# Finer steps for the running sums, a stream's operands made one phase later, and a last projection that stays in PSUM

## The chip, the cores and the metric

The kernel runs on one NeuronCore of a Trainium2 chip, in one launch. Its time is the device time of an execution, in microseconds (us); lower is better. The profile names the engines PE (TensorE matmul; PEld is its weight load), DVE (VectorE), ACT (ScalarE), POOL (GpSimd) and SP (SyncE).

## What is computed

Two blocks of a model, all in float32, on 256 image tokens of width 1024. The first block has two layers with attention, a recurrent branch and a gated feed-forward net. The second has two layers whose shifts, scales and gates come from vectors `c` (and `c_ctx` for a second stream of 256 context tokens); this is the part that the change touches:

```python
def second_block(x, c, ctx, c_ctx, w_ada, b_ada, norm_g, ...):
    h, hc = x, ctx
    for layer in range(DEPTH):                      # 2 layers
        with_ctx = layer < DEPTH - 1                # the context stream leaves after layer 0
        sh_m, sc_m, gt_m, sh_f, sc_f, gt_f = ada_chunks(c, w_ada[layer], b_ada[layer])
        csh_m, ...                         = ada_chunks(c_ctx, w_ada[layer], b_ada[layer])
        xm = modulate(h, g_pre_m, sh_m, sc_m)       # rms norm * (1 + scale) + shift
        cm = modulate(hc, g_pre_m, csh_m, csc_m)
        y, yc = even_mixer(xm, cm, ...) if layer % 2 == 0 else odd_mixer(xm, cm, ...)
        h = h + gt_m * rms_norm_2(y, g_post_m)
        f = conv_ffn(modulate(h, g_pre_f, sh_f, sc_f), w_up[layer], ..., w_down[layer])
        h = h + gt_f * rms_norm_2(f, g_post_f)
        if with_ctx: ...                            # the same two steps for hc
    return h

def ada_chunks(cvec, w, b):                         # w: 1024 x 6144
    m = jax.nn.silu(cvec) @ w + b
    return jnp.split(m[..., None, :], 6, axis=-1)

def odd_mixer(xm, cm, w_qkv, q_g, k_g, w_out, cos, sin, with_ctx):
    # queries of 16 heads from xm; keys and values of 4 heads from xm and cm;
    # norm and rope of queries and keys, softmax attention, @ w_out

def conv_ffn(x, w_up, conv_w, conv_b, w_down):      # 2816 = 22 * 128 hidden channels
    h = conv of 3 tokens over (x @ w_up) + conv_b
    a, g = jnp.split(h, 2, axis=-1)
    return (jax.nn.silu(g) * a) @ w_down
```

## The kernel before

**Products.** Every float32 matrix is split into a high and a low part of the matmul's own type, and a product is three matmuls (`mm3`, L357 to L361): high by high, low by high, high by low. Weights come in 362 blocks of 512 KB and eight of 384 KB (`load`, L324): one DMA on SP's queue into `raw` (3 buffers), ACT copies to `whi`, DVE subtracts to `wlo` (4 buffers each). `self.ahead` blocks are asked for ahead of use. With `self.parts` at 4 the two copies are made in quarters of 128x256.

**Engines.** A tile scheduler places the program's instructions on the engines' queues and puts in semaphore waits. Each queue is then executed in its own order. `high_priority(HP)` lets a piece be placed ahead of what the program wrote before it; `issue_after(i)` holds it back until instruction `i` has been placed, so that it stands behind it.

**Streams.** Stream 0 is the image, stream 1 the context. `prepare` (L1043, its steps from L1047) makes a mixer's or FFN's operands for one stream out of its state `hn` (two tiles of 128 tokens): four ACT squares with row sums (L1056), a reciprocal root of seven small DVE operations for each tile (`rsqrt1`, L410 to L416), four scaled ACT copies (L1061), and for each of eight chunks two PE transposes (L1067), an ACT scale and shift into `pt` (L1070), a DVE cast (L1071) and a DVE subtraction (L1072). `post` (L1075) adds a projection's result to `hn`: two squares (L1080), two products with the gate row (L1084), `rsqrt1`, two updates (L1089).

**Running sums.** The vectors `ada` of the second block are sums over 1024 inputs. For eight of the twelve pieces DVE makes them, while PE does other work: `ada_sums` (L510) loads eight tiles `wadb` of 128x1024 (512 KB, on POOL's DMA queue, 3 buffers), multiplies each by one column for each stream and adds it to `asum` (L524 for the first, L526 for the others). When the eight are done PE sums over partitions (L533, L545) and DVE adds the bias (L535, or L546 and L547 for the gate rows). Four pieces need both streams, and the first four of the eight to be done are these; the last four need stream 0 alone. `ada_sums` is a generator, and yields once for each `wadb` tile; `sum_step` takes steps of it.

**The second block's first FFN** (`second_ffn`, L1230) has 22 hidden chunks in groups of 2, 4, 4, 4, 4 and 4. `up(c)` makes chunk `c` of both streams (48 matmuls of 512 columns into two of four PSUM tiles `up`), and conv, silu and split: on DVE two additions for each half (L1185, L1187), L1219, L1220 and L1094. After the ups of a group, `down` does the products of the group before: 96 matmuls of 512 columns into eight PSUM tiles `acc` (three buffers), each of which DVE adds to `y` (L1271). Sums are taken in each up from the third on: three steps behind the split (L1240 to L1242), which are six sums in a row where both streams are wanted. After the last group, `down` ends with `post` and `prepare` for stream 0 and then for stream 1 (L1261).

**The last mixer** (`odd_mixer`) makes five queries (stream 0 alone, `query`, L1465), two keys of both streams (`keys`, L1439), values, and then attention with three more queries between. A query ends in ACT's `qraw` and `qsq`, four small PE products (L1472), the rope product (L1430), and on DVE L1432 to L1434, L1094 and a root of ten small operations. Its projection (`out_products`, L1144) is done in two halves of four operand chunks: the first in the middle of the attention, copied to `y` by ACT (L1157); the second at the end, added to `y` by DVE (L1160); then `post` and `prepare` of the last FFN.

Of the kernel before, what the change touches and what calls it, by code (L numbers as in the profile page):

```python
# [7 lines left out]
F32 = mybir.dt.float32  # L8
# [11 lines left out]
KD = 8  # L20
# [262 lines left out]
class Net:  # L283
    def __init__(self, tc, I, O):
        self.tc, self.nc, self.I, self.O = tc, tc.nc, I, O
        self.es, self.es2 = ExitStack(), ExitStack()
        pool = lambda name, **k: self.es.enter_context(tc.tile_pool(name=name, **k))
        self.keep = pool("keep", bufs=1)
        self.wp = pool("wp", bufs=4)
        self.sp = pool("sp", bufs=2)  # L290
        self.ps = pool("ps", bufs=1, space=PSUM)
        self.dr = pool("dr", bufs=1, space=bass.MemoryType.DRAM)
        self.loaded = {}
        self.nload = 0
# [12 lines left out]
        self.ada_bufs = 5  # L307

# [15 lines left out]
    def load(self):  # L324
# [9 lines left out]
        for j in range(self.parts):  # L334
            cs = slice(n * j // self.parts, n * (j + 1) // self.parts)
            nc.scalar.activation(hi[:, cs], raw[:, cs], AF.Copy)  # L336
            nc.vector.tensor_tensor(lo[:, cs], raw[:, cs], hi[:, cs].bitcast(F32), op=ALU.subtract)  # L337
# [19 lines left out]
    def mm3(self, out, a, b, start, stop):  # L357
        mm = self.nc.tensor.matmul
        mm(out, a[0], b[0], start=start, stop=False)  # L359
        mm(out, a[0], b[1], start=False, stop=False)  # L360
        mm(out, a[1], b[0], start=False, stop=stop)  # L361
# [43 lines left out]
    def rsqrt1(self, a, b, name):  # L405
# [10 lines left out]
        nc.vector.scalar_tensor_tensor(y, u, R0, y, op0=ALU.add, op1=ALU.mult)  # L416
# [93 lines left out]
    def ada_sums(self):  # L510
# [4 lines left out]
        for u, (l, p) in enumerate(SUMS):  # L515
            streams = (0, 1) if l == 0 or p < 2 else (0,)
            acc = [self.adap.tile([128, 1024], F32, tag="asum", name="asum", bufs=3) for _ in streams]
            for k in range(KD):
# [8 lines left out]
                if k + 1 < KD:  # L527
                    yield
# [22 lines left out]
    def sum_step(self, n=1):  # L551
        for _ in range(n):
            next(self.sum_gen, None)
# [370 lines left out]
    def first_ffn(self, l, gp, other):  # L924
# [10 lines left out]
        def up(c):  # L935
# [14 lines left out]
            if not last and 2 <= c < 2 + KD:  # L950
                with self.tc.issue_after(self.mark.ins):
                    self.sum_step()
# [144 lines left out]
    def second_block(self):  # L1097
        xs = self.xs
        for l in range(DEPTH):
# [3 lines left out]
            with a as mp, b as self.ph:  # L1103
# [8 lines left out]
                with self.tc.high_priority(HP):  # L1112
                    for t in range(2):
                        self.post(t, fin.y(t), B[0], junk, scratch)
                    self.prepare(l, 1, 0, xs, 0, junk, scratch, "sc")
# [57 lines left out]

    def conv_up(self, l, xs, mp, S, between=None):
# [6 lines left out]
        def conv(ps, c, tag):  # L1181
# [5 lines left out]
            nc.vector.scalar_tensor_tensor(a[:, :, :255], b[:, :, 1:], cw[:, 88 + c:89 + c], a[:, :, :255],  # L1187
                                           op0=ALU.mult, op1=ALU.add)
# [12 lines left out]
        def up(c):  # L1201
# [5 lines left out]
            self.parts = 1  # L1207
            if c in held:
# [21 lines left out]
    def second_ffn(self, l, xs, mp, between):  # L1230
# [7 lines left out]
        def up(c):  # L1238
            r = up0(c)
            if c >= 2:  # L1240
                with self.tc.issue_after(self.mark.ins):
                    self.sum_step(3)  # L1242
            return r

        def down(ys, g):
            final = g + 1 == len(FFN2_GROUPS)
            if final:
# [6 lines left out]
                for s in range(2):  # L1254
# [6 lines left out]
                    self.prepare(l + 1, 0, s, nxt, 256 * s, scratch, room, "up")  # L1261
                return
            for i in range(2):
                w = self.weights(len(ys) // 2)
                for t in range(4):
# [4 lines left out]
                    else:  # L1270
                        nc.vector.tensor_tensor(y[t, i], y[t, i], ps, op=ALU.add)  # L1271
# [4 lines left out]
    def second_ffn_last(self, l, xs, mp, B):  # L1276
        y = self.ffn_whole(self.conv_up(l, xs, mp, 1))
        for t in range(2):
            self.post(t, y[t], B[0], lambda: self.chunk(mp, "th", 2), lambda: self.chunk(mp, "a", 2))
# [135 lines left out]
    def odd_mixer(self, xs, mp, streams, scratch):  # L1415
# [67 lines left out]
        for c in range(5):  # L1483
            query(c)
        self.parts = 1
# [6 lines left out]
        for c in range(8):  # L1492
# [7 lines left out]
            elif c == 6:  # L1500
                self.out_products(mp, y, 0, mix, range(2))
        return self.out_products(mp, y, 1, mix, range(2))
# [29 lines left out]
```

## Time and profile before

| | |
|---|---|
| runs | 1716.64, 1718.66 and 1721.53 us, median 1718.66 |
| profiled execution | 1715.54 us, of which the span of the engines' work is 1713.8 |
| PE busy | 1654.7 us, 97% of the span |
| DVE busy | 1261.8 us, 74% |
| ACT busy | 848.1 us, 49% |
| mean granted clock of TensorE | 0.982 |
| chain of work that ended last | PE 84%, DVE 7%, issue 5%, ACT 2%, DMA 1% |

The span is the time from the first to the last recorded instruction. Busy time of PE counts matmuls that run one into the other, so PE at 97% has little left but the stretches in which it stands still or runs at the lower of its two clocks. The chain names what the last instruction waited for, step by step back to the start.

### The profile page before, as it was taken

To read this page: it belongs to the slowest core of one execution; us is meant where nothing else is said; L and a number is where in the kernel's file an instruction comes from. 1 tells how busy PE (TensorE), PEld (TensorE's weight loads), DVE (VectorE), ACT (ScalarE), POOL (GpSimd) and SP (SyncE) were. 2 spreads that over 40 slices of the span, in tenths; PEclk is the share of its full clock that TensorE was granted. 3 is DMA by queue.
4 is the path that set the end of the run, shared out by engine and by line. 5 is a ranking of instruction groups with operands and counts; after the bars stand their busy time and mean duration, and the time that the engine had idled before them with its cause. 6 is when DMAs were issued, how large, how long until landed. Compare 5 with 4: busy or idle time off the path is not lost.

```text
span 1713.8 us, 27366 instructions
## 1 busy us (share of the span) xinstructions
PE 1654.7 (97%) x10336; PEld 1407.6 (82%) x10336; DVE 1261.8 (74%) x2713; ACT 848.1 (49%) x1614; POOL 71.2 (4%) x143
## 2 busy tenths in 40 slices
PE   8999999999989999999999999899999899979998
PEld 7869999998769999996667877677887786669997
DVE  7678986675887766745548898786867977687777
ACT  5575543454756444534556543133332846665554
POOL 0011000000000000000100011010100000000000
PEclk9999999999999999999999999899999999989999
DMA  7446655564356565432223355564642321146663
GB/s 267 157 156 233 217 172 172 166 188 152 101 189 191 184 185 185 143 99 74 72 71 99 111 170 192 163 201 140 215 161 85 119 75 38 62 119 186 186 185 112
DMA packets 71851, 256.77 MB, mean 150 GB/s; under 512 B 8584, under 2 KB 8600, under 8 KB 71720
## 3 DMA queue, kind: packets, MB, share of 16 engines
q1 hardware_dynamic: 56904, 203.58, 37.6%
q0 software_dynamic: 14672, 51.45, 9.2%
q8 instruction: 81, 1.33, 0.3%
q14 instruction: 50, 0.41, 0.1%
q10 hardware_dynamic: 144, 0.00, 0.0%
HBM read 253.92 MB, written 1.07 MB: 149 GB/s over the span
## 4 chain that ended last, share of the span: by engine, by line
PE 84%; DVE 7%; issue 5%; ACT 2%; DMA 1%; POOL 0%; DVEq 0%; POOLq 0%; ACTq 0%
PE acc L359 16%; PE acc L361 16%; PE acc L360 16%; PE up L361 6%; PE up L360 6%; PE up L359 6%; PE sc L1322 3%; PE y L359 2%; PE y L361 2%; PE y L360 2%; PE po L1333 2%; PE pt L1327 2%; DVE wlo L337 2%; PE st L533 1%; DVE asum L526 1%
## 5 line engine op out<-in xcount | busy, mean ns | idle before, releaser
L336 ACT ACTIVATE whi<-raw 128x1024 fp32r<-128x1024 f32 (+2 forms) x439 | 397.4, 919 | 544.7 <-PE acc L360 240.6
L337 DVE TENSOR_TENSOR wlo<-raw,whi 128x1024 fp32r<-128x1024 f32 (+2 forms) x439 | 457.4, 1050 | 204.9 <-ACT whi L336 196.8
L359 PE MATMUL acc<-hi,whi 128*128 128x272 f32 (+1 forms) x848 | 250.3, 295 | 7.8 <-ACT hi L567 7.2
L361 PE MATMUL acc<-hi,wlo 128*128 128x272 f32 (+1 forms) x848 | 248.1, 293 | 0.8 <-DVE wlo L337 0.8
L360 PE MATMUL acc<-lo,whi 128*128 128x272 f32 (+1 forms) x848 | 247.8, 292 | 0.0
L359 PEld LDWEIGHTS acc<-hi,whi 128*128 128x128 f32 x848 | 163.4, 193 | 15.3 <-ACT hi L567 7.2
L359 PE MATMUL acc<-whi,op 128*128 128x512 f32 (+1 forms) x432 | 157.0, 364 | 8.8 <-DVE y L1271 8.4
L360 PEld LDWEIGHTS acc<-lo,whi 128*128 128x128 f32 x848 | 163.4, 193 | 1.6 <-DVE lo L568 0.3
L361 PE MATMUL acc<-op,wlo 128*128 128x256 f32 (+1 forms) x528 | 164.7, 312 | 0.0
L360 PE MATMUL acc<-op,whi 128*128 128x256 f32 (+1 forms) x528 | 164.5, 312 | 0.2 <-DVE op L1072 0.2
L359 PE MATMUL acc<-op,whi 128*128 128x256 f32 (+1 forms) x528 | 164.4, 313 | 0.3 <-ACT qraw L1467 0.3
L361 PEld LDWEIGHTS acc<-hi,wlo 128*128 128x128 f32 x848 | 163.4, 193 | 1.2 <-DVE wlo L337 0.8
L360 PE MATMUL acc<-wlo,op 128*128 128x512 f32 (+1 forms) x432 | 155.2, 360 | 0.0
L360 PE MATMUL up<-op,whi 128*128 128x512 f32 (+1 forms) x384 | 146.2, 381 | 0.0
L359 PE MATMUL up<-op,whi 128*128 128x512 f32 (+1 forms) x384 | 145.6, 381 | 0.2 <-ACT pt L1070 0.2
L361 PE MATMUL up<-op,wlo 128*128 128x512 f32 (+1 forms) x384 | 145.0, 379 | 0.1
L359 PEld LDWEIGHTS acc<-op,whi 128*128 128x128 f32 x528 | 100.0, 190 | 8.7 <-issue 2.2
L360 PEld LDWEIGHTS acc<-op,whi 128*128 128x128 f32 x528 | 101.1, 192 | 6.6 <-issue 1.1
L526 DVE SCALAR_TENSOR_TENSOR asum<-wadb,csp,asum 128x1024 f32<-128x1024 f32 x84 | 104.4, 1277 | 2.1 <-DMA wadb<-wadb 2.1
L361 PEld LDWEIGHTS acc<-op,wlo 128*128 128x128 f32 x528 | 100.1, 190 | 6.3 <-issue 2.1
L359 PEld LDWEIGHTS acc<-whi,op 128*128 128x128 f32 x432 | 82.7, 192 | 25.9 <-DVE y L1271 8.8
L360 PEld LDWEIGHTS acc<-wlo,op 128*128 128x128 f32 x432 | 82.5, 191 | 12.2 <-issue 1.0
(416 smaller groups left out, 3389.9 us busy)
## 6 DMA issues: line engine op xcount, KB each, us to landing
raw<-wts SPq DMA_DIRECT2D x362, 512.0 KB, 3.7
wadb<-wadb POOLq DMA_DIRECT2D x64, 512.0 KB, 4.4
wada<-wada POOLq DMA_DIRECT2D x27, 512.0 KB, 5.6
raw<-wts SPq DMA_DIRECT2D x8, 384.0 KB, 3.1
B<-brow SPq DMA_DIRECT2D x6, 512.0 KB, 3.3
wada<-wada SPq DMA_DIRECT2D x5, 512.0 KB, 6.5
nb<-nbias POOLq DMA_DIRECT2D x16, 128.0 KB, 2.5
h<-xm SPq DMA_DIRECT2D x4, 272.0 KB
```

Source lines behind the costliest of these rows:

```text
L336: nc.scalar.activation(hi[:, cs], raw[:, cs], AF.Copy)
L337: nc.vector.tensor_tensor(lo[:, cs], raw[:, cs], hi[:, cs].bitcast(F32), op=ALU.subtract)
L359: mm(out, a[0], b[0], start=start, stop=False)
L360: mm(out, a[0], b[1], start=False, stop=False)
L361: mm(out, a[1], b[0], start=False, stop=stop)
L526: nc.vector.scalar_tensor_tensor(acc[s], w, c, acc[s], op0=ALU.mult, op1=ALU.add)
L533: nc.tensor.matmul(ps[:, 8 * s + m:8 * s + m + 1], acc[s][:, 128 * m:128 * m + 128], self.ones[:, 0:1], start=True, stop=True)
L1322: mm(ps[i], q[a][rows[i], tok], k[b][rows[i], k0:k0 + nk], start=n == 0, stop=n == 2)
L1327: nc.tensor.transpose(pt[:, 128 * j:128 * j + 128], p[:, 128 * j:128 * j + 128], self.idt)
L1333: mm(po[rows[i]], v[k0 // 128 + j][:, vc:vc + 64], pT[i][j // 2][:, 256 * (j % 2):256 * (j % 2) + 256], start=j == 0, stop=j == nj - 1, ti ...
```

## The change

Four things are changed.

1. `ada_sums` yields after every single sum. In `second_ffn` one sum is taken behind the second addition of each half of an up (L1187, now L1216), one behind its split, and one behind each addition to `y` in the groups' downs. In the first block's first FFN the first 16 single sums are taken one in each up instead of two at a time in eight ups.
2. `prepare` of stream 1 for the last mixer is written in `odd_mixer` behind the five queries, and its transposes are held back until the last product of the fifth query has been placed. They go through PSUM tiles `sc` (2) instead of `up` (4).
3. The last mixer's projection (`out_whole`) leaves its first half in PSUM, three tiles `acc` and one `st`, and adds the second half there. ACT's copies and DVE's additions go. The second half runs token tile by token tile.
4. From `prepare`'s last root in the last layer until the last FFN's second chunk, the DVE half of the next weight blocks (`wlo`) is held back behind that root.

```diff
@@ load
+            with self.tc.issue_after(self.after) if self.after else nullcontext():
+                nc.vector.tensor_tensor(lo[:, cs], raw[:, cs], hi[:, cs].bitcast(F32), op=ALU.subtract)
@@ ada_sums
-                if k + 1 < KD:
-                    yield
+                    if (k, s) != (KD - 1, streams[-1]):
+                        yield
...
-    def sum_step(self, n=1):
-        for _ in range(n):
-            next(self.sum_gen, None)
+    def sum_step(self, after):
+
+        if self.sums_left:
+            self.sums_left -= 1
+            with self.tc.issue_after(after.ins):
+                next(self.sum_gen, None)
@@ first_ffn
-            if not last and 2 <= c < 2 + KD:
-                with self.tc.issue_after(self.mark.ins):
-                    self.sum_step()
+            if not last and c >= 2:
+                self.sum_step(self.mark)
@@ second_block
-                    self.prepare(l, 1, 0, xs, 0, junk, scratch, "sc")
+                    steps = self.prepare_steps(l, 1, 0, xs, 0, junk, scratch, "sc")
+                    next(steps)
+                    if last:
+                        self.after = self.last.ins
+                    for _ in steps:
+                        pass
@@ new
+    def out_whole(self, y, half, mix):
+
+        self.ahead = 2 if half else 3
+        w = self.weights(4)
+        self.ahead = 3
+        halves = (w[:4], w[4:])
+        ms = mix[4 * half:4 * half + 4]
+
+        def tiles(ts):
+            for t, i in ((0, 0), (0, 1), (1, 0), (1, 1)) if half else ((0, 0), (1, 0), (0, 1), (1, 1)):
+                if half == 0:
+                    y[t, i] = self.psum("acc" if (t, i) != (1, 1) else "st")
+                self.gemm_nat(halves[i], ms, slice(128 * t, 128 * t + 128), 512, y[t, i], 0, half == 0, half == 1)
...
@@ conv_up
+            if S == 2:
+                self.sum_step(m)
...
+            if c == 1:
+                self.after = None
@@ second_ffn
-            if c >= 2:
-                with self.tc.issue_after(self.mark.ins):
-                    self.sum_step(3)
+            if c == 1:
+                self.sums_left = 100
+            elif c >= 2:
+                self.sum_step(self.mark)
...
-                    self.prepare(l + 1, 0, s, nxt, 256 * s, scratch, room, "up")
+                    if s == 0:
+                        self.prepare(l + 1, 0, 0, nxt, 0, scratch, room, "up")
...
-                        nc.vector.tensor_tensor(y[t, i], y[t, i], ps, op=ALU.add)
+                        self.sum_step(nc.vector.tensor_tensor(y[t, i], y[t, i], ps, op=ALU.add))
@@ odd_mixer
         for c in range(5):
             query(c)
+        with self.tc.high_priority(HP):
+            steps = self.prepare_steps(1, 0, 1, xs, 256, lambda: self.chunk(mp, "p", 3), scratch, "sc")
+            next(steps)
+            with self.tc.issue_after(self.product.ins):
+                for _ in steps:
+                    pass
...
-                self.out_products(mp, y, 0, mix, range(2))
-        return self.out_products(mp, y, 1, mix, range(2))
+                self.out_whole(y, 0, mix)
+        self.parts = PARTS
+        return self.out_whole(y, 1, mix)
```

Further lines keep the handles that these need (`self.product`, the last matmul of `mm3`; `self.last`, the last operation of `rsqrt1`), and give the final `post` other scratch tiles. In the changed kernel lines stand some three to 35 further down.

On DVE in the first FFN of the second block, at a chunk whose sums want both streams (`asum` is the running sum, `a` and `g` the two halves of a chunk, `pl` its split, `y` a down's result), the order before is:

```order
1636 L1094 SCALAR_TENSOR_TENSOR pl<-g,op 128x512
1637 L526 SCALAR_TENSOR_TENSOR asum<-wadb,csp,asum 128x1024 x6
1638 L1187 SCALAR_TENSOR_TENSOR a<-up,par,a 128x2x255
1639 L1187 SCALAR_TENSOR_TENSOR g<-up,par,g 128x2x255
1640 L337 TENSOR_TENSOR wlo_12223<-raw_12220,whi_12222 128x1024
1641 L1219 SCALAR_TENSOR_TENSOR g<-th,g 128x512
1642 L1271 TENSOR_TENSOR y<-y,acc 128x512
1643 L1220 TENSOR_TENSOR g<-g,a 128x512
1644 L1271 TENSOR_TENSOR y<-y,acc 128x512 x2
1645 L1094 SCALAR_TENSOR_TENSOR pl<-g,op 128x512
1646 L526 SCALAR_TENSOR_TENSOR asum<-wadb,csp,asum 128x1024 x6
```

and now, in the same down:

```order
1720 L340 TENSOR_TENSOR wlo_12644<-raw_12641,whi_12643 128x1024
1721 L1214 SCALAR_TENSOR_TENSOR g<-up,par,g 128x2x255
1722 L1306 TENSOR_TENSOR y<-y,acc 128x512
1723 L1216 SCALAR_TENSOR_TENSOR g<-up,par,g 128x2x255
1724 L529 SCALAR_TENSOR_TENSOR asum<-wadb,csp,asum 128x1024
1725 L1252 SCALAR_TENSOR_TENSOR g<-th,g 128x512
1726 L529 SCALAR_TENSOR_TENSOR asum<-wadb,csp,asum 128x1024
1727 L1253 TENSOR_TENSOR g<-g,a 128x512
1728 L1306 TENSOR_TENSOR y<-y,acc 128x512 x2
1729 L1099 SCALAR_TENSOR_TENSOR pl<-g,op 128x512
1730 L529 SCALAR_TENSOR_TENSOR asum<-wadb,csp,asum 128x1024
```

Six sums in a row have become single ones, and the additions to `y` now have one sum between them.

On PE at the end of the first three queries of the last mixer (`whi_14336` before, and `whi_14240` now, is the weight block of the fourth query; `qsq` the first query's squares; `con` by `pl` or `qkv` a transpose), before:

```order
7226 L361 MATMUL acc<-op,wlo_13887 128x256
7227 L1067 MATMUL up<-con_139,pl 128x128 x16
7228 L359 MATMUL acc<-op,whi_14336 128x256
7229 L360 MATMUL acc<-op,whi_14336 128x256
7230 L361 MATMUL acc<-op,wlo_14337 128x256
7231 L359 MATMUL acc<-op,whi_14336 128x256
7232 L360 MATMUL acc<-op,whi_14336 128x256
7233 L361 MATMUL acc<-op,wlo_14337 128x256
7234 L359 MATMUL acc<-op,whi_14336 128x256
7235 L1472 MATMUL st<-con_139,qsq 128x2 x2
```

and now:

```order
7226 L364 MATMUL acc<-op,wlo_13887 128x256
7227 L362 MATMUL acc<-op,whi_14240 128x256
7228 L363 MATMUL acc<-op,whi_14240 128x256
7229 L364 MATMUL acc<-op,wlo_14241 128x256
7230 L362 MATMUL acc<-op,whi_14240 128x256
7231 L363 MATMUL acc<-op,whi_14240 128x256
7232 L1507 MATMUL st<-con_139,qsq 128x2 x2
7233 L1465 MATMUL st<-qraw,pgq 128x256
```

The 16 transposes have left this place; the first query's small products (L1472, now L1507) and its rope product (L1430, now L1465) stand five matmuls behind the three queries. The transposes now stand 55 rows further down, among the products of the first key block.

ACT's queue there, as changed: the squares of stream 1 (L1056, now L1061) stand ahead of the first query's copies.

```order
913 L338 ACTIVATE whi_14309<-raw_14307 128x256 x4
914 L338 ACTIVATE whi_14378<-raw_14376 128x256 x2
915 L1061 ACTIVATE p,pss<-hn_6335 128x512 x2
916 L1061 ACTIVATE p,pss<-hn_6337 128x512 x2
917 L1502 ACTIVATE qraw<-acc 128x256 x2
918 L1504 ACTIVATE qsq<-qraw 128x256 x2
919 L338 ACTIVATE whi_14378<-raw_14376 128x256
920 L1066 ACTIVATE qkv<-hn_6335,pr 128x512 x2
```

The six weight copies, four squares and two `qraw` are now what PE's L1507 stands behind.

## Rows read from the trace of the kernel before

**Rows 1.** The page: the span, and busy time by engine.

```profile
span 1713.8 us, 27366 instructions
PE 1654.7 (97%) x10336; PEld 1407.6 (82%) x10336; DVE 1261.8 (74%) x2713; ACT 848.1 (49%) x1614; POOL 71.2 (4%) x143
```

**Rows 2.** Timeline of PE, 1077 to 1087 (start, duration, instruction, idle before).

```profile
1076.41 0.40 PE L360 MATMUL acc<-wlo,op 128*128 128x512 f32 x1
...
1077.34 0.40 PE L361 MATMUL acc<-whi,pl 128*128 128x512 f32 x1
1086.12 0.80 PE L359 MATMUL acc<-whi,op 128*128 128x512 f32 x1 [8.38 <-DVE y L1271]
```

**Rows 3.** Busy time by stretch; last PE's granted clock, DMA share, GB/s.

```profile
core 0: us, PE busy (x) PEld busy (x) DVE busy (x) ACT busy (x) POOL busy (x), PEclk, DMA share, GB/s
1086.10:1091.40 5.30, 5.28 (x12) 4.15 (x13) 5.30 (x7) 1.69 (x2) 0.25 (x1) 0.50 0.33 95
...
1352.80:1360.80 8.00, 3.83 (x16) 1.91 (x17) 7.12 (x31) 7.74 (x20) 0.00 (x0) 0.81 0.68 201
1360.80:1364.40 3.60, 3.60 (x17) 3.60 (x18) 3.46 (x13) 2.65 (x7) 0.00 (x0) 0.50 0.70 226
1501.10:1511.60 10.50, 0.02 (x1) 0.02 (x1) 10.34 (x42) 6.13 (x17) 0.00 (x0) 0.66 0.32 99
1511.60:1518.10 6.50, 5.52 (x24) 4.68 (x25) 3.42 (x11) 5.00 (x9) 0.00 (x0) 0.50 0.27 83
```

**Rows 4.** Timeline of DVE, 1075 to 1086.

```profile
1075.16 7.25 DVE L526 SCALAR_TENSOR_TENSOR asum<-wadb,csp,asum 128x1024 f32<-128x1024 f32 x6
...
1085.38 0.68 DVE L1271 TENSOR_TENSOR y<-y,acc 128x512 f32<-128x512 f32 x1
```

**Rows 5.** Groups of DVE, 945 to 1325 (count; busy, mean ns; idle before).

```profile
L526 DVE SCALAR_TENSOR_TENSOR asum<-wadb,csp,asum 128x1024 f32<-128x1024 f32 x70 | 87.0, 1277 | 2.1 <-DMA wadb<-wadb 2.1
L337 DVE TENSOR_TENSOR wlo<-raw,whi 128x1024 fp32r<-128x1024 f32 x58 | 70.6, 1219 | 30.0 <-ACT whi L336 29.8
L1271 DVE TENSOR_TENSOR y<-y,acc 128x512 f32<-128x512 f32 x32 | 21.6, 682 | 16.8 <-PE acc L361 16.6
L1185 DVE SCALAR_TENSOR_TENSOR a<-up,par,a 128x510 f32<-128x510 f32 x22 | 16.3, 743 | 0.2 <-ACT a L1183 0.2
...
L1219 DVE SCALAR_TENSOR_TENSOR g<-th,g 128x512 f32<-128x512 f32 x22 | 15.1, 687 | 7.9 <-ACT th L1218 7.9
```

**Rows 6.** Timeline of PE, 1352 to 1377.

```profile
1352.51 0.28 PE L361 MATMUL acc<-op,wlo 128*128 128x256 f32 x1
1354.20 0.66 PE L1067 MATMUL up<-con,pl 128*128 128x128 f32 x4 [1.42 <-ACT pl L1061]
...
1360.80 0.58 PE L359 MATMUL acc<-op,whi 128*128 128x256 f32 x1 [0.26 <-ACT qraw L1467]
...
1376.44 0.68 PE L1430 MATMUL st<-qraw,pgq 128*128 128x256 f32 x2
```

**Rows 7.** Timeline of ACT, 1350 to 1353.

```profile
1350.67 0.73 ACT L336 ACTIVATE whi<-raw 128x256 fp32r<-128x256 f32 x2 [1.36 <-PE acc L360]
1351.30 0.62 ACT L1056 ACTIVATE th<-hn 128x512 f32<-128x512 f32 x1
...
1352.53 1.01 ACT L336 ACTIVATE whi<-raw 128x256 fp32r<-128x256 f32 x3
```

**Rows 8.** Timeline of PE, 1500 to 1512.

```profile
1500.70 0.39 PE L361 MATMUL acc<-whi,op 128*128 128x512 f32 x1
1511.58 0.69 PE L1067 MATMUL sc<-con,qkv 128*128 128x128 f32 x2 [10.49 <-ACT qkv L1061]
```

**Rows 9.** Timeline of DVE, 1508 to 1514.

```profile
1508.84 1.22 DVE L337 TENSOR_TENSOR wlo<-raw,whi 128x1024 fp32r<-128x1024 f32 x1
...
1513.92 0.29 DVE L1071 CAST op<-pt 128x256 fp32r<-128x256 f32 x1 [2.38 <-ACT pt L1070]
```

**Rows 10.** Timeline of ACT, 1502 to 1514.

```profile
1502.01 0.61 ACT L1080 ACTIVATE p<-y 128x512 f32<-128x512 f32 x1
...
1510.81 2.56 ACT L1061 ACTIVATE qkv<-hn,pr 128x512 f32<-128x512 f32 x4 [1.60 <-DVE pr L416]
1513.32 1.02 ACT L1070 ACTIVATE pt<-sc,ada,der 128x256 f32<-128x256 f32 x2
```

**Rows 11.** DMA issues, 945 to 1330 (count, KB, us to landing).

```profile
raw<-wts SPq DMA_DIRECT2D x62, 512.0 KB, 3.8
wadb<-wadb POOLq DMA_DIRECT2D x53, 512.0 KB, 4.6
```

**Rows 12.** Busy time of the 20 us with the most traffic of 945 to 1330.

```profile
1140.00:1160.00 20.00, 20.00 (x81) 14.29 (x80) 17.26 (x22) 6.61 (x9) 3.14 (x6) 1.00 0.70 237
```

More of the change, by code (lines that the diff above doesn't have):

```diff
@@ L1 @@
 import math
-from contextlib import ExitStack
+from contextlib import ExitStack, nullcontext
 import concourse.bass as bass
@@ L307, in __init__ @@
         self.ada_bufs = 5
+        self.after = None
+        self.sums_left = 2 * KD
     def con(self, pool, i):
@@ L336, in load @@
             nc.scalar.activation(hi[:, cs], raw[:, cs], AF.Copy)
-            nc.vector.tensor_tensor(lo[:, cs], raw[:, cs], hi[:, cs].bitcast(F32), op=ALU.subtract)
+            with self.tc.issue_after(self.after) if self.after else nullcontext():
+                nc.vector.tensor_tensor(lo[:, cs], raw[:, cs], hi[:, cs].bitcast(F32), op=ALU.subtract)
         v = lambda t: t.rearrange("p (k m) -> p k m", k=nk)
@@ L360, in mm3 @@
         mm(out, a[0], b[1], start=False, stop=False)
-        mm(out, a[1], b[0], start=False, stop=stop)
+        self.product = mm(out, a[1], b[0], start=False, stop=stop)
     def gemm(self, w, m, xs, cols, n, ps=None):
@@ L415, in rsqrt1 @@
         nc.vector.scalar_tensor_tensor(u, t, -R1, t, op0=ALU.add, op1=ALU.mult)
-        nc.vector.scalar_tensor_tensor(y, u, R0, y, op0=ALU.add, op1=ALU.mult)
+        self.last = nc.vector.scalar_tensor_tensor(y, u, R0, y, op0=ALU.add, op1=ALU.mult)
         return y
@@ L1172, in out_products @@
         return tiles
+    def out_whole(self, y, half, mix):
[9 more added lines that the diff above has]
+                self.gemm_nat(halves[i], ms, slice(128 * t, 128 * t + 128), 512, y[t, i], 0, half == 0, half == 1)
+        tiles.y = lambda t: [y[t, 0], y[t, 1]]
+        if half == 0:
+            tiles((0, 1))
+        return tiles
     def conv_up(self, l, xs, mp, S, between=None):
@@ L1186, in conv @@
                                            op0=ALU.mult, op1=ALU.add)
-            nc.vector.scalar_tensor_tensor(a[:, :, :255], b[:, :, 1:], cw[:, 88 + c:89 + c], a[:, :, :255],
-                                           op0=ALU.mult, op1=ALU.add)
+            m = nc.vector.scalar_tensor_tensor(a[:, :, :255], b[:, :, 1:], cw[:, 88 + c:89 + c], a[:, :, :255],
+                                               op0=ALU.mult, op1=ALU.add)
+            if S == 2:
+                self.sum_step(m)
             return t
@@ L1207, in up @@
             self.parts = 1
+            if c == 1:
+                self.after = None
             if c in held:
@@ L1278, in second_ffn_last @@
         for t in range(2):
-            self.post(t, y[t], B[0], lambda: self.chunk(mp, "th", 2), lambda: self.chunk(mp, "a", 2))
+            self.post(t, y[t], B[0], lambda: self.chunk(mp, "th", 2), lambda: self.chunk(mp, "ag"[t], 2))
             for i in range(2):
```

## The prediction

> **What bounds the kernel now.** I read the page first: PE is busy for 1654.7 of 1713.8 us [rows 1]. So an edit can only gain where PE stands still, or runs at its lower clock. A timeline of PE alone, read for idle times over 0.3 us, gives three such places near the change, and each is then read on the engine that PE waits for.
>
> Place A is the one long stop in the second block's first FFN: PE waits 8.38 us for an addition to `y`, L1271 [rows 2]. DVE shows why: six sums stand in a row from 1075.16 for 7.25 us, and two conv additions, a weight block and one more operation come before the addition that PE needs, which starts at 1085.38 [rows 4]. When PE starts again the granted clock is 0.50, the lower of its two levels (1.2 GHz): twelve matmuls take 5.3 us [rows 3].
>
> Place B is the start of the last mixer. The last of the three first queries' matmuls starts at 1352.51, the next query product at 1360.80; between them are only the 16 transposes of stream 1, waiting for ACT's copies [rows 6]. PE is busy for 3.83 of 8.00 us there, and the next 3.60 us are at 0.50 [rows 3].
>
> Place C is the end of the last mixer: PE waits 10.49 us for `prepare` [rows 8], then 6.50 us are at 0.50 [rows 3].
>
> **The change, A.** PE's pitch for 512 columns at full clock is (1077.34 - 1076.41) / 4 = 0.233 us [rows 2]. A sum holds DVE for 1.28 us, a weight block 1.22, a conv addition 0.74, L1219 (and L1220 and L1094, which have its shape) 0.69, an addition to `y` 0.68 [rows 5]. Of the changed order, an up has 2 blocks, 4 conv additions, 3 of the L1219 kind and 3 sums: 2.44 + 2.97 + 2.06 + 3.83 = 11.3 us of DVE, against 48 x 0.233 = 11.2 us of PE. Before, an up with both streams had six sums: 15.1 us. A down has 4 blocks, 8 additions and 8 sums, 4.88 + 5.46 + 10.22 = 20.5 us, against 96 x 0.233 = 22.4. Four ups and a down: DVE 65.8 us, PE 67.1. DVE keeps up, just; and no addition to `y` stands behind more than two sums (2.6 us), where three `acc` buffers of 2.8 us of PE each are its slack.
>
> So the stop goes: 8.38, and of the twelve slow matmuls 5.3 - 12 x 0.233 = 2.5, together 10.9. I put 1 us against it for small new waits, since DVE has 1.3 us in 67 to spare: **-10**. Bounds: -11 (no wait), -5 (half of it comes back as short waits). The number of sums is the same, and so is its DVE time, before as after. In the first block's FFN the same sums are singly placed where PE has no stop to lose: 0.
>
> **B.** The 16 transposes leave PE's stop. What can be won: 1360.8 - 1352.6 = 8.2 us, less 1.9 for the transposes themselves, which are still to be done (four take 0.66, of which about 0.28 is the last one's own length [rows 6]: 0.12 each), and the slow stretch after it, 3.6 us at half speed, 1.8 of it lost [rows 3]: 8.1 in all. But a new wait takes its place. PE's queue now has the first query's small products L1472 five matmuls (0.6 us) behind the three queries, at 1353.2. They need `qsq`, which on ACT stands behind six weight quarters, four squares and two `qraw`. ACT can begin the quarters at 1350.67, when the first query's block is free; two squares with their quarters' return take 1352.53 - 1351.30 = 1.23, a quarter about 0.33 (three begin 1352.53 and last 1.01) [rows 7]. So 1350.67 + 6 x 0.33 + 2.46 + 2 x 0.3 + 0.35 = 1356.1: a wait of 2.9 us. Behind it stand the rest of the fourth and all of the fifth query's matmuls, none of which needs it. Late next are the chunks of stream 1: DVE has the ropes and roots of the fourth and fifth query before and among their casts, and the first key needs all eight. From 1356.1: 43 query products of 256 columns at half of 0.233 are 5.0, three queries' small products and ropes 2.7 (an estimate of 0.9 each, a rope alone taking 0.68 [rows 6]), and the start at the lower clock 1.8 (half of place B's 3.6 us); then 24 key products of 0.233, 16 transposes and the last two queries' small products: 5.6 + 1.9 + 1.8. That ends near 1375. Before, at 1376.44, six of the key's 24 products were still to come [rows 6], an end near 1378.5. **-3.5**. Bounds: 0 (DVE's casts come later by as much), -8.1 (all is covered).
>
> The clock here: PE's waits of 8.38 and of 10.49 us are both followed by rows at 0.50, and so are the scattered ones of place B, 4.2 us in sum [rows 2, 3, 8]. The Trainium skill (TensorE: Matmul & The Clock Gate, HAM oscillation) says that a kernel whose matmuls keep pausing for their data falls back to the slow clock at every pause and pays for the change each time. The rows of B agree with that. By it the new wait is paid as above, -3.5; if the wait is too short to lose the clock, the sum for B would be -5.3.
>
> **C.** The second half's products end at the same place (24 matmuls at 0.233 after the last of the attention). What changes is behind them. The first token tile's two results are ready some 12 matmuls earlier; four additions on DVE (0.68, as L1271 [rows 5]), and four ACT copies in the middle of the attention that hid under PE, are gone. The last square (L1080) then starts at 1501.5 instead of 1502.01 [rows 10]. DVE no longer has a block of 1.22 us [rows 9] and eight quarters of 0.33 between the roots, which begin only after the last root. Worked through on the changed queues (ACT: square, block 1.0, four squares of `hn` at 0.62 [rows 7] with a wait for L1089, root, four copies 2.56): the first `pt` at 1510.9 to 1511.4 instead of 1513.32 [rows 10]. The two blocks held back, 1.22 + 1.13, now stand ahead of the first cast: about 1512.1 instead of 1513.92 [rows 9]. **-1.8**. Bounds: -0.3 (the `st` tile's late result and ACT's order eat it), -4 (the blocks find a gap). The slow stretch of 6.50 us behind the stop stays.
>
> **Sum.** -10 - 3.5 - 1.8 = -15.3. The profiled execution took 1715.54 us (1713.8 plus 1.74 around it), 3.1 under the median of the runs, 1718.66. So the profiled time becomes about 1700.2, and the median **1703.4**. A measurement of this kernel tells 0.3%, some 5.2 us, from no change.
>
> **Rivals.**
> (1) More than forecast. ACT reaches `qsq` before PE does, so B gives its whole 8.1, and the blocks of C hide, -4: -10.9 - 8.1 - 4 = -23, 1695.7. For it: ACT was idle for 1.36 us before 1350.67 [rows 7]. Against it: its order has twelve instructions there that nothing skips.
> (2) DVE stays the bound. It was idle 30 us for `whi` and 17 for `acc` in this stretch [rows 5]. Where ACT's weight copies come late in the new order too, DVE's 1.3 us in 67 don't cover it. 5 us lost in each of the two or three groups with sums take back 10 to 15: -15.3 + 12 = -3, 1715, no change that could be told. For it: the margins. Against it: before, ups with 15.1 us of DVE for 11.2 of PE stopped PE for long only once.
> (3) Slower: sums that wait for their own tile. The last 32 sums want stream 0 alone, and each has its own `wadb`. In a down there are now eight, and four weight blocks: 12 x 0.524 MB in 22.4 us is 281 GB/s, where the busiest 20 us so far moved 237 [rows 12]. A tile needs 4.6 us to land [rows 11] and there are three buffers. A sum that waits on DVE holds the additions behind it, and these hold PE. If each of the 32 comes late by x, the kernel loses 32x and wins 15.3; it is slower by over 5.2 from x = 0.64 us. At 1 us: +17, 1735. Against it: before, sums waited for a tile for 2.1 us in all [rows 5], and a mean of the order of [rows 12] in so short a stretch is not yet a limit that any row shows. The Trainium skill (PSUM — Partial Sum Buffer, Engine vs sequencer instructions) has the queues of VectorE and ScalarE as strictly first in, first out, so nothing passes such a wait; the stop of place A, with `y` behind six sums, agrees.
>
> **How the numbers follow.** The forecast with its bounds (1698 to 1710) 0.62; rival 1 0.14; rival 2 0.17, half of it within 0.3%, the rest faster by less than forecast; rival 3 0.07. Faster: 0.62 + 0.14 + 0.07 = 0.83. Same: 0.10. Slower: 0.07. The range leaves out rival 3, the end of 1 and the last part of 2: 1694 to 1714.
>
> **What would show it.** A right: no PE wait over 2 us for L1306 (the additions' new line), PE at full clock through 1050 to 1320; wrong: DVE rows `asum` with idle before them for DMA `wadb`. B right: PE's idle before L1507 near 3 us, with clock 0.50 after, and the first key's last product some 3.5 us nearer to the last down; wrong: idle before key products for `op`. C right: PE's stop before the transposes near 8.5 us instead of 10.49. The prediction fails most likely by A: if waits for L1306 or L1252 add up to more than 3 us, it is rival 2.

## The result, and the profile after

The changed kernel takes 1698.12 us (median of 4 runs, 1693.81 to 1699.28), the kernel before 1717.65 (4 runs beside it): a ratio of 0.9885, 95% interval 0.9859 to 0.9911. That is 19.5 us less, where 15.3 were forecast. Four further runs of the same kernel (1695.08 to 1698.79) make it 1696.7 over all eight.

The page of the changed kernel, span and busy times, to be read beside [rows 1]:

```profile
span 1696.0 us, 27339 instructions
PE 1648.7 (97%) x10336; PEld 1403.1 (83%) x10336; DVE 1261.8 (74%) x2706; ACT 848.4 (50%) x1607; POOL 70.4 (4%) x143
```

DVE's busy time is the same to the tenth. The four additions of the last projection are gone, and the group of the sums holds DVE 2.4 us longer (89.4 below, 87.0 in [rows 5]); the other work was only placed elsewhere. PE's busy time is 6 us less with the same 10336 matmuls, which is time at the lower clock; the other 12 us of the span are idle time.

Two rows of PE cut both programs into the same stretches: one among the transposes for the second block's first FFN, and one among those for the last mixer's stream 0. The kernel before:

```profile
926.05 0.44 PE L1067 MATMUL sc<-con,qkv 128*128 128x128 f32 x2 [1.24 <-ACT pt L1070]
1339.88 0.66 PE L1067 MATMUL up<-con,pl 128*128 128x128 f32 x4 [1.09 <-ACT pl L1061]
```

and the changed kernel, with PE's stop before the last FFN as third row (in [rows 8] for before):

```profile
925.73 0.44 PE L1072 MATMUL sc<-con,qkv 128*128 128x128 f32 x2 [1.23 <-ACT pt L1075]
1325.92 0.66 PE L1072 MATMUL up<-con,pl 128*128 128x128 f32 x4 [1.08 <-ACT pl L1066]
1493.40 0.69 PE L1072 MATMUL sc<-con,qkv 128*128 128x128 f32 x2 [7.11 <-ACT qkv L1066]
```

Place A's stretch (first row to second) went from 413.83 to 400.19, -13.6. Place B's (second row to the start of the stop, 1511.58 - 10.49 and 1493.40 - 7.11) from 161.21 to 160.37, -0.8. Place C's (from there to the end of the span) from 212.71 to 209.71, -3.0. With 0.3 ahead of the first row these are the 17.8 us between the spans.

**A.** From its second product on PE's only idle time over 0.35 us in the first FFN is now this row:

```profile
1074.67 0.50 PE L362 MATMUL up<-op,whi 128*128 128x512 f32 x1 [0.67 <-ACT whi L338]
```

and DVE's groups, beside [rows 5], no longer wait for a tile, and wait longer for ACT's weight copies (40.1 us where it was 30.0), that is, DVE is early:

```profile
L529 DVE SCALAR_TENSOR_TENSOR asum<-wadb,csp,asum 128x1024 f32<-128x1024 f32 x70 | 89.4, 1278 | 0.1
L340 DVE TENSOR_TENSOR wlo<-raw,whi 128x1024 fp32r<-128x1024 f32 x58 | 70.9, 1223 | 40.1 <-ACT whi L338 39.7
```

**B.** PE in the changed kernel, from the last product of the three queries:

```profile
1339.26 0.28 PE L364 MATMUL acc<-op,wlo 128*128 128x256 f32 x1
1342.15 0.58 PE L362 MATMUL acc<-op,whi 128*128 128x256 f32 x1 [2.61 <-ACT qraw L1502]
...
1343.38 0.85 PE L1507 MATMUL st<-con,qsq 128*128 128x2 f32 x4
```

and ACT before that (the last of the four squares, then the first query's two copies and their squares):

```profile
1341.12 0.62 ACT L1061 ACTIVATE p<-hn 128x512 f32<-128x512 f32 x1
...
1341.73 0.63 ACT L1502 ACTIVATE qraw<-acc 128x256 f32<-128x256 f32 x2
1342.26 0.72 ACT L1504 ACTIVATE qsq<-qraw 128x256 f32<-128x256 f32 x2
```

PE doesn't get as far as L1507. It stops at the fourth query's first product, which needs one of the three `acc` tiles, and these hold the three queries until ACT's `qraw` has copied one. That copy stands behind the four squares. After the wait the stretch of 6.8 us is at the lower clock:

```profile
1342.10:1348.90 6.80, 6.75 (x30) 6.55 (x30) 3.40 (x21) 4.63 (x11) 0.00 (x0) 0.51 0.19 66
```

**C.** PE's stop is 7.11 us instead of 10.49. The blocks held back stand on DVE between the last root and the first cast, which waits for nothing but them (beside [rows 9]); ACT's first `pt`, one of the two in the first row (beside [rows 10]), is there 0.4 us before that cast:

```profile
1495.58 1.02 ACT L1075 ACTIVATE pt<-sc,ada,der 128x256 f32<-128x256 f32 x2
1494.18 2.36 DVE L340 TENSOR_TENSOR wlo<-raw,whi 128x1024 fp32r<-128x1024 f32 x2
1496.45 0.49 DVE L1076 CAST op<-pt 128x256 fp32r<-128x256 f32 x2
```

### The profile page after: what moved, and what is told of

Its sections match the earlier page's. It is cut to its first block, busy times and chain, and to the rows that moved or that the text cites. A ratio compares the mean times of both kernels' runs of the same rounds, so it can differ in the third digit from the quotient of the medians.

```text
span 1696.0 us, 27339 instructions
## 1 busy us (share of the span) xinstructions
PE 1648.7 (97%) x10336; PEld 1403.1 (83%) x10336; DVE 1261.8 (74%) x2706; ACT 848.4 (50%) x1607; POOL 70.4 (4%) x143
## 4 chain that ended last, share of the span: by engine, by line
PE 81%; issue 10%; DVE 5%; ACT 2%; DMA 1%; POOL 0%; DVEq 0%; SPq 0%; POOLq 0%; ACTq 0%
PE acc L362 15%; PE acc L363 15%; PE acc L364 15%; PE up L362 6%; PE up L363 6%; PE up L364 6%; PE sc L1357 2%; PE y L362 2%; PE y L363 2%; PE y L364 2%; PE po L1368 2%; PE pt L1362 2%; DVE wlo L340 1%; DMA wada<-wada 1%; PE st L536 1%
## 5 line engine op out<-in xcount | busy, mean ns | idle before, releaser
L364 PEld LDWEIGHTS acc<-hi,wlo 128*128 128x128 f32 x848 | 161.9, 191 | 1.2 <-DVE wlo L340 0.8
L362 PE MATMUL acc<-whi,op 128*128 128x512 f32 (+1 forms) x424 | 151.0, 357 | 0.4 <-ACT op L1098 0.4
L363 PE MATMUL acc<-wlo,op 128*128 128x512 f32 (+1 forms) x424 | 150.2, 355 | 0.0
```

The lines of the kernel that those rows point to most:

```text
L364: self.product = mm(out, a[1], b[0], start=False, stop=stop)
```

## The experiments

Each is told by the three stretches of its profile, cut at the same rows, since what lies ahead of the first row alone moves the span by over 6 us from one execution to the next (that row stands at 923.1 to 929.6 us). The stretches vary too where no edit touches them: A takes 412.1 to 414.5 us in the four profiles with the sums as before, B 161.2 and 162.1 (before, and the sums alone), C 212.7 to 213.1. Times are medians; the kernel before, run beside each, had 1717.7 to 1718.6.

| kernel | time, us | A | B | C |
|---|---|---|---|---|
| before | 1717.65 | 413.8 | 161.2 | 212.7 |
| changed | 1698.12 | 400.2 | 160.4 | 209.7 |
| sums alone | 1703.36 | 400.1 | 162.1 | 213.1 |
| stream 1 later, alone | 1714.46 | 414.3 | 158.5 | 212.9 |
| projection, no hold-back | 1715.81 | 414.5 | 161.9 | 212.0 |
| projection and hold-back | 1715.52 | 412.1 | 162.8 | 210.4 |
| changed, squares later | 1691.87 | 400.2 | 155.4 | 210.2 |
| changed, six sums in each up | 1733.20 | 435.0 | 159.8 | 209.2 |
| changed, three in a row | 1696.77 | 401.2 | 158.2 | 209.5 |
| changed, two tile buffers | 1702.16 | 406.9 | 160.0 | 209.3 |
| changed, six in every second up | 1703.98 | 406.2 | 162.3 | 210.1 |
| squares later, three in a row | 1695.52 | 405.9 | 154.7 | 209.5 |
| changed, again | 1695.38 | 400.4 | 160.4 | 209.7 |

**One part at a time.** Four kernels, each the kernel before with one part of the diff.

*The sums* (ratio 0.9916, 0.9902 to 0.9931).

> The kernel before with the finer steps of the running sums alone. Theory (the stop of 8.38 us, the slow clock behind it, the 1.6 us of slow clock behind the two sets of small bias products that stood close together, and a 0.8 us wait for a gate row all go because no more than two sums stand in a row): the first FFN of the second block is some 13 us shorter and nothing else moves, 1704 to 1706 us where the kernel before takes 1718. Rival (part of this gain comes from the other edits): 1708 to 1712.

Measured: 14.3 us less, a little more than the theory's 12 to 14; A is 400.05. The gain is all A's, as the theory had it.

*Stream 1's operands* (ratio 0.9986, 0.9973 to 0.9999).

> The kernel before with stream 1's operands made behind five queries, alone. Theory (PE's stop for the transposes is replaced by a wait of 2.6 us for the first query's copy, which ACT makes behind four squares, and by a longer stretch at the lower clock): 0 to 2 us faster than before. Rival, the prediction's term: 3.5 us faster, the new wait being behind and the clock lost for 3.6 us only.

Measured: B 158.5, 2.7 less than before, between the two; against the profile of the sums alone, whose B no edit touches either, it is 3.5 less, so the two cases are not told apart. PE's wait is there to the hundredth, but what follows it is not at the lower clock:

```profile
1359.73 0.38 PE L359 MATMUL acc<-op,whi 128*128 128x256 f32 x1 [2.61 <-ACT qraw L1468]
```

```profile
1359.70:1366.50 6.80, 6.76 (x53) 6.66 (x54) 6.07 (x37) 6.23 (x17) 0.00 (x0) 1.00 0.23 80
```

53 matmuls in 6.8 us at 1.00, where the changed kernel did 30 at 0.51. The clock falls later instead, some 33 us behind the wait, for 3.4 us:

```profile
1393.20:1396.50 3.30, 3.30 (x17) 3.30 (x16) 2.77 (x13) 0.38 (x1) 0.00 (x0) 0.50 0.00 0
```

*The last projection*, without the hold-back (ratio 0.9996, 0.9984 to 1.0007) and with it (0.9994, 0.9982 to 1.0006). The times are inside the noise, so the stops decide.

```diff
 # without the hold-back: load() and prepare() as before
-        return self.out_products(mp, y, 1, mix, range(2))
+        self.parts = PARTS
+        return self.out_whole(y, 1, mix)
```

> The kernel before with the last projection accumulated in PSUM, without the hold-back of the next weight blocks. Theory (the shorter chain on DVE and ACT is most of it): PE's stop of 10.49 us becomes 7.5 to 8.5 and the kernel is 1.5 to 2.5 us faster. Rival (the hold-back does it): no more than 0.7 us faster, the weight block still standing between the roots.

> The kernel before with the last projection in PSUM and the hold-back. Theory: PE's stop near 7.1 us, 2.9 us faster than before, and 0.5 to 1 us faster than without the hold-back. Rival (the blocks held back, 2.36 us on DVE, stand in front of the first cast and cost what they give): same as without it or slower.

PE without the hold-back, and with it:

```profile
1509.39 0.69 PE L1067 MATMUL sc<-con,qkv 128*128 128x128 f32 x2 [8.94 <-ACT qkv L1061]
```

```profile
1508.81 0.47 PE L1069 MATMUL sc<-con,qkv 128*128 128x128 f32 x1 [7.25 <-ACT qkv L1063]
```

Without it, DVE has whole blocks between the roots and the updates:

```profile
1504.08 1.22 DVE L337 TENSOR_TENSOR wlo<-raw,whi 128x1024 fp32r<-128x1024 f32 x1
...
1506.50 1.41 DVE L1089 SCALAR_TENSOR_TENSOR hn<-qkv,yr,hn 128x512 f32<-128x512 f32 x2
```

So the stop gives 1.6 by the projection and 1.7 by the hold-back; C is 0.8 and then 2.3 shorter. The theory on the first missed: the stop is above its 8.5 and C gives less than its 1.5, hardly more than the rival's 0.7. On the second, the rival that the held blocks cost what they give is out by the stop, which is 7.10 to 7.11 us in all eight profiles with both parts in the changed kernel; the kernels' times cannot tell the two apart.

**Is it the row of six, or the number in an up?** The prediction read the stop of place A as six sums standing in a row ahead of an addition. Three kernels take the changed one and alter only where its sums are taken.

```diff
 # six in each up: two behind each of the two conv halves, two behind the split
+                self.sum_step(m)
                 self.sum_step(m)
 # and none in the downs
-                        self.sum_step(nc.vector.tensor_tensor(y[t, i], y[t, i], ps, op=ALU.add))
+                        nc.vector.tensor_tensor(y[t, i], y[t, i], ps, op=ALU.add)
```

> The changed kernel with six sums in each up, two at each of the three places, and none in the downs: DVE has as much to do in an up as before, 15.1 us for 11.2 of PE. Theory (what stopped PE was six sums in one row ahead of the additions): no stop over 1.5 us, within 3 us of the changed kernel. Rival (it was the DVE load of an up, whatever its order): stops of 5 to 9 us in the ups whose sums want both streams, 8 to 12 us slower than the changed kernel.

```diff
 # three in a row behind the split (second kernel: six, where c is even)
-            if S == 2:
-                self.sum_step(m)
...
-                self.sum_step(self.mark)
+                for _ in range(3):
+                    self.sum_step(self.mark)
```

> The changed kernel with the three sums of an up in one row behind its split, the downs as changed. Theory (three in a row are 3.8 us, and four PSUM tiles of an up, or three of a down, give 5.6 us or more of slack): waits of under 1 us, within 2 us of the changed kernel, so that the number in each up counts and their spreading inside it does not. Rival (the spreading counts): stops of 1 to 3 us in several ups, 4 to 10 us slower.

> The changed kernel with six sums in one row behind the split of every second up, none in the ups between, the downs as changed: the row of the kernel before at the changed kernel's rate. Theory (what stopped PE before was that four ups in a row ask DVE for 15.1 us each while PE needs 11.2; a row of six at half the rate is caught up in the next up): no stop over 2 us, within 4 us of the changed kernel. Rival, the prediction's reading (the row of six itself stops PE, standing ahead of the addition to y): stops of 3 to 8 us before L1305, 6 to 20 us slower than the changed kernel.

Six in each up, at most two in a row: A is 435.0, 21 us longer than before the change, and the whole kernel slower than before (ratio 1.0095, 1.0064 to 1.0126). PE has two stops:

```profile
1087.83 0.80 PE L362 MATMUL acc<-whi,op 128*128 128x512 f32 x1 [11.34 <-DVE y L1308]
1183.06 1.20 PE L536 MATMUL st<-con,asum 128*128 128x1 f32 x5 [12.04 <-DVE asum L529]
```

and DVE, ahead of the first, needs 13.87 us from one up's split to the next, where PE needs 11.2 for its products:

```profile
1060.47 0.69 DVE L1099 SCALAR_TENSOR_TENSOR pl<-g,op 128x512 fp32r<-128x512 f32 x1
...
1074.34 0.69 DVE L1099 SCALAR_TENSOR_TENSOR pl<-g,op 128x512 fp32r<-128x512 f32 x1
```

That is 2.7 us behind in an up; were it so in each of the four ups of a group (an estimate from this one), it would be 10.7, and the stop is 11.34. Three in a row at three in each up cost nothing that the times show (1696.77; A 401.2). Six in a row at the same rate cost some: 1703.98, A 406.2, with these two stops the longest, and DVE waiting for tiles for 3.2 us in all:

```profile
1070.40 0.50 PE L362 MATMUL acc<-whi,op 128*128 128x512 f32 x1 [1.22 <-DVE y L1305]
...
1219.41 0.79 PE L362 MATMUL acc<-whi,op 128*128 128x512 f32 x1 [2.59 <-DVE y L1305]
```

DVE ahead of the two:

```profile
1057.29 7.25 DVE L529 SCALAR_TENSOR_TENSOR asum<-wadb,csp,asum 128x1024 f32<-128x1024 f32 x6
...
1216.86 0.17 DVE L538 TENSOR_TENSOR ada<-st,par 128x8 f32<-128x8 f32 x1 [1.44 <-PE st L536]
```

Only the first stop, of 1.22 us, has a row of six ahead of it. Ahead of the second the sums stand singly between other work, one of them waits 0.39 us for its tile, and DVE waits 1.44 us for PE's own bias products. So the number in an up decides; that a row of six costs more than those 1.22 us where the rate is right is not shown. With six in each up the theory (the row) fell and its rival (the load) stood, at 35 us instead of 8 to 12, since PE's bias products stopped for a late sum as well and PE ran at the lower clock around both stops. With six in every second up neither case held: 5.9 us over the changed kernel (7.3 over the median of its eight runs) is past the theory's 4, one stop is over its 2, and both are below the rival's 3.

The load is not all of the stop before the change. DVE waited in that stretch too, for the bias products that PE makes of two finished sums:

```profile
1064.78 0.17 DVE L535 TENSOR_TENSOR ada<-st,par 128x8 f32<-128x8 f32 x1 [1.30 <-PE st L533]
...
1067.77 0.17 DVE L535 TENSOR_TENSOR ada<-st,par 128x8 f32<-128x8 f32 x1 [2.16 <-PE st L533]
```

With six in each up there are such waits as well (1.29 and 2.37 us before 1056). No run takes them away alone, so their share of the 8.38 us is open.

**Squares later.** The changed kernel with stream 1's squares held back until ACT has squared the first two queries.

```diff
-            next(steps)
+            with self.tc.issue_after(copied[1].ins):     # the second query's square
+                next(steps)
```

> The changed kernel with stream 1's four squares placed behind the squares of the first two queries on ACT. Theory (PE's 2.61 us wait before the fourth query is for a PSUM tile that ACT's copy of the first query frees, and this copy stands behind the four squares): the wait falls under 0.8 us, and the slow clock behind it goes or gets shorter, 3 to 6 us faster than the changed kernel. Rival (the operands of stream 1 then come later by as much, and the first key waits for them): the wait moves to the key, 0 to 1 us.

1691.87 us (1690.61 to 1693.81), ratio to before 0.9855 (0.9833 to 0.9877), and B is 155.4, 5.0 less than the changed kernel's. PE, at the fourth query's first product and at the one stop that is left:

```profile
1336.97 0.39 PE L362 MATMUL acc<-op,whi 128*128 128x256 f32 x1 [0.16 <-ACT qraw L1504]
...
1345.71 0.44 PE L1072 MATMUL sc<-con,qkv 128*128 128x128 f32 x2 [0.55 <-ACT pt L1075]
```

```profile
1336.70:1343.50 6.80, 6.64 (x53) 6.47 (x53) 5.76 (x31) 6.80 (x22) 0.00 (x0) 1.00 0.44 157
```

The wait was ACT's order, and the first key did not wait instead: of the 5.0 us, 2.3 are idle time of PE, and 3.3 the lower clock behind the wait, against 0.6 of other matmul time. This is the fastest kernel of the study.

**The tiles.** The changed kernel with `bufs=2` for `wadb`.

> The changed kernel with two buffers for the sums' tiles instead of three. Theory (a tile lands in 4.6 us and a sum is asked for every 2.8 to 3.7 us, so a third buffer is what keeps the single-stream sums from waiting): waits of DVE for tiles appear in the last units, 10 to 25 us in all, and PE loses 3 to 15 us. Rival (transfers are far from the limit): no wait over 1 us, no change.

1702.16, A 406.9, 6.7 longer than with three. DVE's waits for tiles, and PE's stop at the bias products of a finished sum:

```profile
DVE asum L529 <- DMA wadb<-wadb: 4.3, 5, 1.6
```

```profile
1245.82 0.35 PE L536 MATMUL st<-con,asum 128*128 128x1 f32 x2 [2.10 <-DVE asum L529]
```

The waits are smaller than expected (10 to 25), the loss in the range. Of the 6.7, 1.8 is idle time of PE and the rest the lower clock, 1.7 of it at the operands of the first FFN, which the edit does not touch. So rival 3's waits exist, one buffer away, though the kernel is still some 16 us faster than before the change. With three buffers the traffic came to what rival 3 reckoned with (281 GB/s in a down), and no sum waited for it:

```profile
1220.00:1240.00 20.00, 20.00 (x95) 16.49 (x95) 16.71 (x21) 3.75 (x4) 3.71 (x7) 1.00 0.84 280
```

**Both.** Squares later, and three sums in a row.

> The changed kernel with stream 1's squares behind the first two queries' squares and the three sums of an up in one row. Theory: as with the squares alone, 1690 to 1693 us, since the row of three changed nothing and the squares took away the only new wait. Rival (the two edits' gains add up to more than that): under 1689 us.

1695.52, not what either case said: B has its gain (154.7), but A is 405.9 in the profile, which is of the slowest of the four runs (1700.43; two others took 1693.5). There, at the bias products of the same sum as with two buffers, three sums in a down waited for tiles, two of them for

```profile
1236.56 1.28 DVE L529 SCALAR_TENSOR_TENSOR asum<-wadb,csp,asum 128x1024 f32<-128x1024 f32 x1 [1.79 <-DMA wadb<-wadb]
...
1241.90 1.28 DVE L529 SCALAR_TENSOR_TENSOR asum<-wadb,csp,asum 128x1024 f32<-128x1024 f32 x1 [1.66 <-DMA wadb<-wadb]
```

and PE stopped 3.23 us at the bias products. With the same rows of three, the kernel without the squares' move had 0.9 us of such waits. That the rows of three bring it and not chance in the transfers is not shown; the two runs near 1693.5 make chance likelier.

**Again.** The changed kernel, profiled once more.

> The changed kernel as it is, profiled a second time. Theory (the 2.61 us wait before the fourth query brings the lower clock in some executions and not in others): the wait is again 2.61 us, and the stretch from the first transposes of stream 0 to the end of the second half's products takes either about 160.2 us, with some twelve slow matmuls behind the wait, or about 158.3 us without them. Rival (the lower clock always follows, and the kernels in which it didn't differ in something else): 160.0 to 160.6 us again.

B 160.4, the lower clock after the wait again (30 matmuls in 6.8 us, 0.52). So the theory that it varies between executions of this kernel found no support in two profiles of it. Over the profiles with the wait of 2.60 to 2.62 us, it is followed by the lower clock in five and by the full clock in two (stream 1 alone, and three in a row, whose B are 158.5 and 158.2). In both of the two the clock falls 33 us later, as shown above for the first; of the five only one has such a fall too, 51 us behind its wait (six in every second up, B 162.3). What makes the difference stays open.

## Why the prediction was right, and where it was off

The forecast, 1703.4, was 5 us too slow, inside its range, with the right sign for every term.

**A was mis-sized, and its reading was wrong in part.** Forecast -10, with -11 as the most that could be; measured -13.6. The stop and the twelve slow matmuls went, 11.0 in all, and the 1 us set against it came out as 1.4: 0.7 for the one new stop, the rest in smaller pieces. What the step left out: a wait of 0.7 us of PE for a gate row's DVE work, and 1.7 us lost at the lower clock behind two sets of 16 small bias products (L533), which stood 3 us apart and stand 4.8 apart now, with no fall of the clock in the 9 us around them:

```profile
1062.90 1.84 PE L533 MATMUL st<-con,asum 128*128 128x1 f32 x16
...
1065.87 1.86 PE L533 MATMUL st<-con,asum 128*128 128x1 f32 x16
1067.60:1071.00 3.40, 3.40 (x9) 2.73 (x10) 3.23 (x5) 0.00 (x0) 0.53 (x1) 0.51 0.24 69
```

Another 1.6 is lower clock at the operands of the first FFN (6.1 us of matmuls then, 3.0 now). No edit touches these, and the kernel with two tile buffers has 6.4 there, so this part is luck. The step "six sums in a row from 1075.16" took the last thing that DVE did before the addition for the cause. The table of DVE and PE time in an up, 15.1 against 11.2, stood in the same prediction and was the cause, as far as the runs separate the two: the kernel with six in each up, two in a row, stops longer than before.

**B had its mechanism right, one place off.** Forecast -3.5; measured -0.8 in this profile and -2.7 where it was done alone. The wait was put at 2.9 us before L1507 for `qsq`; it is 2.61, before the fourth query, for the tile that `qraw` frees. The step had no term for that tile. The same squares stand ahead of both on ACT. PE's busy time in the whole of B, before, now, and with the sums alone, where no edit touches B:

```profile
1339.88:1501.09 161.21, 155.79 (x896) 113.08 (x896) 117.60 (x396) 103.97 (x261) 0.00 (x0) 0.98 0.21 68
1325.92:1486.29 160.37, 156.20 (x896) 114.52 (x896) 117.26 (x400) 102.47 (x257) 0.00 (x0) 0.97 0.22 68
1325.12:1487.17 162.05, 156.61 (x896) 114.38 (x896) 117.77 (x396) 103.86 (x261) 0.00 (x0) 0.97 0.22 68
```

Idle time fell by 1.25 us, from 5.42 to 4.17. Of the matmul time 1.5 us went and 2.0 came back as lower clock: 10.0 us of matmuls at 0.50 instead of 6.1. The step set the loss behind the new wait at 1.8, equal to that at the old place; they were 3.3 and 3.0, both mis-sized, but the one still pays for the other. The other 1.7 came from lower clock behind stream 0's first transposes, which no edit touches. The profile of the kernel before has none there, that of the sums alone has it, and its B is 162.1; so -0.8 is partly bad luck, and -1.7 against the sums alone is the like comparison. Idle time and matmuls without the clock gave 2.8 of the 3.5; the 0.7 between is not traced. It is not the first key's wait: behind the wait for `qraw` PE has no idle time over 0.25 us in B.

The Trainium skill (TensorE: Matmul & The Clock Gate, HAM oscillation) tells of a kernel whose waits for data, longer than this one, each brought the slow clock. Here the wait of 2.6 us is followed by it in five profiles and not in two. In these two B came to -2.7 and -3.0, where the sum without the loss was -5.3: they have the later fall of the clock, 1.7 lost, and the rest of the difference stays open.

**C was right and too small.** Forecast -1.8; measured -3.0. The step had the held blocks in the right place and at about the right cost: the first cast comes 0.4 us behind the end of ACT's first `pt`, though the blocks take 2.36. It mis-sized the chain of roots ahead of them. Counted from the end of the second half's products, `pt` begins 9.3 us behind it instead of 12.2, 2.9 earlier where the forecast had 1.9 to 2.4, and the cast comes 2.7 earlier where it had 1.8. The blocks' leaving the roots is half of the gain.

**The rivals.** The first (more than forecast) came half true: A and C passed their forecast, B did not reach it. The second (DVE stays the bound) is what the kernel with six in each up does; in the changed kernel DVE waits 40 us for weights. The third (tiles too late, slower) did not happen: its traffic came, 280 GB/s over 20 us, and its waits did not. (The 237 of [rows 12] is the most of stretches cut at every 20 us; from 1138 to 1158 the kernel before moved 259.) Two buffers bring such waits, and the kernel with both edits had 4.2 us of them. The Trainium skill (PSUM — Partial Sum Buffer, Engine vs sequencer instructions) has VectorE's queue as first in, first out; the rows of that kernel agree: PE's last product for two of the additions to `y` ended at 1233.3 us, and DVE started them at 1237.77 and 1239.56, behind a sum that began at 1236.56 after its wait for a tile.

## What to carry to other kernels

Compare the work that each unit of a loop asks of two engines before looking for the instruction that stands ahead of the stop: a lag of 2.7 us in a unit, in several units in a row, went with a stop of 11 us, and neither of the two orders tried at that load helped. Where a piece of work is moved behind other work, look for it in the queue of every engine that it uses: four squares that ACT could have done a moment later cost PE 2.6 us and, in five of seven profiles, its clock right behind, and moving these alone gave 5 us in that stretch. Price work that is held off a chain by what the chain waits for at its new place, not by its length. And before a difference of 1 or 2 us in a stretch is put down to an edit, compare profiles in which no edit touches that stretch: here such profiles differ by 0.4 to 2.4 us.

## What was not expected of the hardware

A wait of PE of 2.60 to 2.62 us in seven profiles was followed at once by 6.8 us at the lower clock in five; in two the clock fell only 33 us later, for 3.4 us. Two sets of 16 bias products of one column, about 1.84 us each, often follow each other on PE with a few other matmuls between. With 2.9 to 3.2 us from one start to the next, the lower clock set in during the second set or within 2 us behind it, without a stop of PE, in 10 of 14 cases over all profiles; with 3.6 to 5.7 us, in none of 24. The two sets that lie in the first block are among these: 3.1 us apart with the old placing of the sums (the lower clock in three of four profiles), 5.7 with the new (in none of nine), so that this place gained too, though the forecast had put it at 0. That the distance is the cause was not tried by itself.
